# One decoder trunk step on one core: two convolution blocks as three pairs of column blocks, and half of the low parts by an accumulating transfer

## The chip, the core and the metric

The kernel runs on one core of a Trainium2 chip. A core has a matrix engine (TensorE, PE in the profile, with its weight loads as PEld), a vector engine (VectorE, DVE), an activation engine (ScalarE, ACT), a general engine (GpSimd, POOL) and a queue engine (SyncE, SP) that only starts transfers. Transfers run on 16 DMA engines; SP and POOL start nearly all of them here. The metric is the device time of one execution, in microseconds (us).

## What is computed

One step of a decoder layer for 512 prompt positions and 8 sample tokens, 520 columns in all, with a model width of 2048. The core of the reference:

```python
def mixer(xn, conv_prev, gla_prev, w_in, conv_w, gate_w2, gate_b, gla_norm_g, w_out, chunk):
    proj = xn @ w_in                       # 2048 -> 6160 columns
    bg, cg, hin, q, k, v, og, glr = jnp.split(proj, [_S1, _S2, _S3, _S4, _S5, _S6, _S7], axis=-1)
    cu, conv_new = causal_dwconv(cg * hin, conv_prev, conv_w)
    ya = bg * cu                           # 1024 channels of gated convolution
    logf = jax.nn.log_sigmoid((glr @ gate_w2 + gate_b).astype(f32)) / GATE_TAU
    o, s_new = gla_chunked(qh, kh, vh, lf, gla_prev.astype(f32), chunk)   # 4 heads
    ...
    yb = (o.reshape(Bn, L, GLA_V_DIM) * jax.nn.silu(og.astype(f32))).astype(xn.dtype)
    out = jnp.concatenate([ya, yb], axis=-1) @ w_out

def trunk(...):
    m, c_new, s_new = mixer(rmsnorm(x, norm_mix_g[l]), ...)
    x = x + m
    f, f_new = conv_ffn(rmsnorm(x, norm_ffn_g[l]), ...)   # 2048 -> 2 x 5632 -> 2048
    x = x + f
    return rmsnorm(x, final_norm_g), ...
```

The 1024 convolution channels are 8 blocks of 128. A block j needs three blocks of 128 columns of the input projection: one of cg, one of hin and one of bg.

## The kernel before

**Products in three parts.** All matrices are float32. A weight tile of 128 x 1024 (eight 128 x 128 pieces of one column block, 512 KB) is loaded as `raw`, rounded by ScalarE to `hi`, and VectorE subtracts `lo = raw - hi`. The activations are split likewise, and a product is hi x hi + lo x hi + hi x lo: three matmuls, each of 128 x 128 weights against 260 columns (half of the 520).

**Stages.** Up to about 59 us the input is transposed and split. Then comes the *plain stage*: column blocks of the input projection one after the other, each by `group()` (L213): 16 pieces in depth, three parts, two halves of the columns, 96 matmuls. After it comes the *pair stage*: two column blocks at once by a seven-product scheme (the products named in `ORDER`; sums of the weights and sums of the activations go in, and each of the seven products has half the depth and half the columns), 7 x 8 x 3 = 168 matmuls for what takes two plain groups 192. The output projection and the two FFN projections use the seven products as well.

**The plain stage** has 28 column blocks from 59 us on: the value blocks of head 0, four blocks (key, query, two of value) of each of heads 1 to 3 with one convolution block (`conv_tile`, three groups) behind each, the fourth convolution block, and two output-gate blocks (columns 5120 and 5248, in code of their own after the loop, L1797 to L1830). Within it the linear attention of a head is a generator (`gla_head`, L934). It is cut into small steps, and `group()` lets one step go at each of its *beats*, after the depth pieces named in `BEATS`: at 3, 7, 11 and 15. A step puts a few small matmuls between those of the group and gives VectorE, ScalarE and POOL the work that belongs to it. A level of the attention runs like this: POOL subtracts cumulative gates (`e`, L285), ScalarE takes the exponential (L984), VectorE multiplies with query and key into `L` (L991), TensorE forms scores of it (L1066), VectorE copies these into `at` (L1073). Products run two steps ahead of their scores and the subtractions three. `mixer_sums` (L774), another generator, prepares activation sums for the pair stage, one step at the end of each group.

**Weights of the plain stage.** Two halves (eight depth pieces each) make a block. `next_half()` (L205) takes a finished half and calls `high()` (L190), in which ScalarE makes the `hi` of the half that is used two halves later. Three pieces into the half, `low()` (L197) lets VectorE make its `lo`, and `fetch()` (L185) starts the load of the half three further on, from SP. Each of `raw`, `hi` and `lo` has three buffers, so a load waits until the `lo` of the half that had the buffer is made, and `hi` waits until TensorE is through with the half three before.

**Order.** In this part of the program every engine, with POOL's and SP's queues, keeps the order in which the code was written (`InOrder`, L885). An instruction that waits holds all behind it on its engine.

**The pair stage** goes through `MIX`: `ch` is the cg and hin blocks of one convolution block, `b` the bg blocks of two convolution blocks, `og` two output-gate blocks. Each pair takes `prepare` (L1355) for hi and lo of the weight sums, and one of the sums is made by an accumulating transfer from POOL's queue (`raw<-raw`, L1319). The results of convolution blocks are stored as `g_d`, from where the output projection loads them.

Of the kernel before, what the change touches and what calls it, by code (L numbers as in the profile page):

```python
# [17 lines left out]
P = 128  # L18
# [19 lines left out]
def trunk_kernel(  # L38
# [146 lines left out]
    def fetch():  # L185
        if ahead:
            k0, c0 = ahead.popleft()
            coming.append(load(w_in, k0, 8, c0, P))

    def high():  # L190
        if coming:
            raw, nk = coming.popleft()
            hi = wp.tile([P, 1024], F32R, tag="hi", name="hi")
            nc.scalar.activation(hi, raw, AF.Copy)
            highs.append((raw, nk, hi))

    def low():  # L197
        if highs:
            raw, nk, hi = highs.popleft()
            lo = wp.tile([P, 1024], F32R, tag="lo", name="lo")  # L200
            nc.vector.tensor_tensor(lo, raw, hi.bitcast(F32), op=ALU.subtract)
            halved.append([x.rearrange("p (k c) -> p k c", k=nk) for x in (hi, lo)])
            fetch()
# [7 lines left out]
    BEATS = (3, 7, 11, 15)  # L211

    def group():  # L213
        ps = new_mm()
        for k in range(KD):
            if k % 8 == 0:
                w = next_half()
            span(ps, w, xa, k, k // 8 * 8, 1, KD)
            if k in BEATS:
                beat()  # L220
            if k % 8 == 3:
                low()
        if extra and next(extra[0], extra) is extra:
            extra.popleft()
        return ps
# [548 lines left out]
    def mixer_sums():  # L774
# [38 lines left out]
        ("ch", 4), ("og", 2), ("ch", 5), ("og", 4), ("b", 4), ("og", 6), ("ch", 6), ("ch", 7),  # L813
        ("b", 6),
# [26 lines left out]
    with ExitStack() as mix:  # L841
# [44 lines left out]
        with ExitStack() as gl:  # L886
# [15 lines left out]
            for h in range(NH):  # L902
                tile_cols = (3584 + h * P, 3072 + h * P, 4096 + h * DV, 4096 + h * DV + P)
                for c0 in (*tile_cols, *(x + (h - 1) * P for x in (1024, 2048, 0)))[
                    slice(3, 4) if h == 0 else slice(None)
                ]:
                    ahead += [(0, c0), (8, c0)]
            ahead += [(k0, c0) for c0 in (1408, 2432, 384, 5120, 5248) for k0 in (0, 8)]
# [324 lines left out]
            for h in range(NH):  # L1233
                if h == 1:
                    extra.append(mixer_sums())
                ps = group() if h else None
# [3 lines left out]
                ps = group() if h else None  # L1240
# [23 lines left out]
                if h:  # L1264
                    conv_tile(h - 1)
            conv_tile(NH - 1)
# [838 lines left out]
```

## Time and profile before

| what | value |
|---|---|
| median of 3 runs | 2143.29 us (2142.72 to 2144.54) |
| the profiled execution's own time | 2143.29 us |
| its span, first to last instruction | 2141.5 us |
| granted TensorE clock, mean | 0.998 |
| TensorE busy | 2117.8 us, 99% |
| VectorE / ScalarE / POOL busy | 1747.0 / 1105.2 / 434.9 us |

The profiled execution is the median run. A matmul row of 281 ns is not the price of a matmul: matmuls overlap, and the price is the distance between their starts, which is read from the chain of waits or from the timeline. Stages are best told apart by a table of windows: it gives the busy time of each engine in each stretch, the granted clock, the share of the DMA engines, and what they moved.

### The profile page before, as it was taken

The numbers are of one execution on the slowest core, as the hardware profiler recorded it, in microseconds if no ns is written. First come the engines' busy times: TensorE is split into PE (matmuls) and PEld (weight loads), VectorE is DVE, ScalarE is ACT, GpSimd is POOL, SyncE is SP. The second block draws the span as 40 slices with busy tenths as digits, with TensorE's granted clock in tenths as the row PEclk, the third lists the DMA queues.
The fourth block names the chain that finished last, engine by engine and source line by source line (L and its number), as shares of the span: only waits on it lengthen the run. The fifth ranks groups of instructions, "written<-read, shape, count | busy, mean of one in ns | idle before, by whom it ended". The sixth has DMA issues, their size and how long they took to land.

```text
span 2141.5 us, 44283 instructions
## 1 busy us (share of the span) xinstructions
PE 2117.8 (99%) x17952; PEld 2097.2 (98%) x17952; DVE 1747.0 (82%) x2333; ACT 1105.2 (52%) x1662; POOL 434.9 (20%) x622
## 2 busy tenths in 40 slices
PE   9999999999999989999999999999999999999997
PEld 8999999999999989999999999999999999999997
DVE  6457576688979898998998988988989778888886
ACT  7434434355544686555555555555555554444445
POOL 4213223111334311111211221212212300200000
PEclk9999999999999999999999999999999999999999
DMA  8445473597898996676676676676676966994734
GB/s 257 129 134 176 132 206 114 147 253 187 223 287 239 267 287 164 173 190 177 179 185 174 181 184 174 180 187 175 178 188 180 298 203 163 276 291 133 225 109 159
DMA packets 467325, 415.74 MB, mean 194 GB/s; under 512 B 21721, under 2 KB 426473, under 8 KB 466977
## 3 DMA queue, kind: packets, MB, share of 16 engines
q1 hardware_dynamic: 424209, 289.84, 47.7%
q0 software_dynamic: 42864, 123.00, 21.9%
q8 instruction: 141, 2.31, 0.4%
q14 instruction: 63, 0.52, 0.1%
q10 hardware_dynamic: 48, 0.07, 0.0%
HBM read 299.65 MB, written 80.31 MB: 177 GB/s over the span
## 4 chain that ended last, share of the span: by engine, by line
PE 87%; DMA 5%; DVE 4%; issue 2%; POOL 1%; ACT 1%; SPq 1%; ACTq 0%; DVEq 0%; POOLq 0%
PE mm L1394 34%; PE mm L140 15%; PE ms L1394 14%; PE x L1637 7%; PE y L1637 7%; PE f L1637 3%; PE e L1637 3%; DVE lo L1374 1%; DMA x_d<-acc 1%; DMA form<-g_d 1%; DMA raw<-in_w_in_dram 1%; DMA wgraw<-in_w_in_dram 1%; DVE acc L1656 1%; PE ms L1066 1%; DMA g_d<-fh 0%
## 5 line engine op out<-in xcount | busy, mean ns | idle before, releaser
L1394 PE MATMUL mm<-yl,hi 128*128 128x260 f32 x1696 | 477.2, 281 | 3.5 <-DVE yl L124 3.5
L1394 PE MATMUL mm<-yh,hi 128*128 128x260 f32 x1696 | 475.9, 281 | 1.3 <-ACT ms L1404 0.7
L1394 PE MATMUL mm<-yh,lo 128*128 128x260 f32 x1696 | 475.3, 280 | 1.4 <-DVE lo L1374 1.4
L1370 ACT ACTIVATE hi<-raw 128x1024 fp32r<-128x1024 f32 x324 | 341.8, 1055 | 242.2 <-issue 90.1
L1374 DVE TENSOR_TENSOR lo<-raw,hi 128x1024 fp32r<-128x1024 f32 x324 | 396.1, 1222 | 44.3 <-ACT hi L1370 40.8
L1374 DVE TENSOR_TENSOR lo<-s,hi 128x1024 fp32r<-128x1024 f32 x243 | 298.5, 1228 | 124.4 <-ACT hi L1370 124.2
L1370 ACT ACTIVATE hi<-s 128x1024 fp32r<-128x1024 f32 x243 | 256.7, 1056 | 220.6 <-PE ms L1394 93.6
L1394 PEld LDWEIGHTS mm<-yl,hi 128*128 128x128 f32 x1696 | 318.9, 188 | 4.1 <-DVE yl L124 4.1
L1394 PEld LDWEIGHTS mm<-yh,lo 128*128 128x128 f32 x1696 | 319.9, 189 | 1.8 <-DVE lo L1374 1.8
L1394 PEld LDWEIGHTS mm<-yh,hi 128*128 128x128 f32 x1696 | 319.8, 189 | 1.7 <-ACT ms L1404 0.9
L1394 PE MATMUL ms<-b,hi 128*128 128x260 f32 x1408 | 265.7, 281 | 0.0
L1394 PEld LDWEIGHTS ms<-b,hi 128*128 128x128 f32 x1408 | 222.8, 189 | 0.0
L1637 PE MATMUL x<-form,hi 128*128 128x260 f32 x1120 | 211.8, 281 | 0.9 <-ACT f L1662 0.5
L1637 PE MATMUL y<-form,hi 128*128 128x260 f32 x1120 | 211.5, 281 | 0.0
L1315 DVE TENSOR_TENSOR s<-s,raw 128x1024 f32<-128x1024 f32 x162 | 198.0, 1222 | 2.8
L1394 PE MATMUL ms<-b,lo 128*128 128x260 f32 x704 | 197.4, 280 | 0.0
L1637 PEld LDWEIGHTS x<-form,hi 128*128 128x128 f32 x1120 | 176.5, 188 | 1.7 <-issue 0.8
L1637 PEld LDWEIGHTS y<-form,hi 128*128 128x128 f32 x1120 | 176.5, 188 | 0.3
L1637 PE MATMUL x<-form,lo 128*128 128x260 f32 x560 | 157.0, 280 | 0.4 <-DVE lo L1374 0.4
L1637 PE MATMUL y<-form,lo 128*128 128x260 f32 x560 | 156.8, 280 | 0.0
L1394 PEld LDWEIGHTS ms<-b,lo 128*128 128x128 f32 x704 | 132.4, 188 | 0.0
L1394 PE MATMUL mm<-bh,hi 128*128 128x260 f32 x424 | 118.8, 280 | 1.0 <-DVE acc L1656 1.0
(402 smaller groups left out, 5005.1 us busy)
## 6 DMA issues: line engine op xcount, KB each, us to landing
raw<-in_w_up_dram SPq DMA_DIRECT2D x176, 512.0 KB, 5.1
raw<-in_w_down_dram SPq DMA_DIRECT2D x96, 512.0 KB, 5.6
raw<-in_w_in_dram SPq DMA_DIRECT2D x92, 512.0 KB, 4.3
form<-f_d SPq DMA_DIRECT2D x126, 260.0 KB, 6.1
raw<-raw POOLq DMA_DIRECT2D x56, 512.0 KB, 5.9
f_d<-t POOLq DMA_DIRECT2D x80, 260.0 KB, 5.5
raw<-in_w_out_dram SPq DMA_DIRECT2D x32, 512.0 KB, 9.3
form<-g_d POOLq DMA_DIRECT2D x42, 260.0 KB, 7.6
```

What stands on the lines that cost most here:

```text
L140: nc.tensor.matmul(o, w, xx, start=first and i == 0, stop=last and i == 2)
L1066: nc.tensor.matmul(pb[t, c * 32 : (c + 1) * 32], L[:, c, t], second(L[:, c : c + 1, t])[:, 0], start=True, stop=True, tile_position=(0, t. ...
L1315: return lambda: nc.vector.tensor_tensor(out, x, y, op=ALU.add)
L1370: nc.scalar.activation(his[i], src, AF.Copy)
L1374: nc.vector.tensor_tensor(los[i], src, his[i].bitcast(F32), op=ALU.subtract)
L1394: nc.tensor.matmul(st["bank"][b], w[:, k, :], x, start=b not in st["used"] and k == 0 and j == 0, stop=k == 7 and j == 2, skip_group_check ...
L1637: nc.tensor.matmul(ps[:, m, :], w[:, k, m * P : (m + 1) * P], x, start=b not in st["used"] and k == 0 and j == 0, stop=k == 3 and j == 2, ...
L1656: nc.vector.tensor_tensor(a, a, inner(bk[b]), op=op)
```

## The change

Four things change together.

- Convolution blocks 2 and 3 leave the plain stage, which so has 22 column blocks in place of 28. They come back as three pairs at the head of `MIX`: `ch` 2, `ch` 3 and `b` 2. Blocks 0 and 1 stay plain and stand together behind head 3.
- `BEATS` has five entries (2, 5, 8, 11, 14), so the steps of a head come after three depth pieces in place of four, and a head's steps are spread over four groups and a little.
- `mixer_sums` goes on twice in the key and query groups, in the middle and at the end.
- For the second half of each block (`k0 == 8`, 21 halves in all) VectorE makes no `lo`. ScalarE writes the negative of `hi` into the `lo` buffer right after `hi`, and POOL starts a transfer that adds `raw` to it.

```diff
--- before.py
+++ after.py
@@ -185,20 +185,26 @@
     def fetch():
         if ahead:
             k0, c0 = ahead.popleft()
-            coming.append(load(w_in, k0, 8, c0, P))
+            coming.append((*load(w_in, k0, 8, c0, P), k0 == 8))
 
     def high():
         if coming:
-            raw, nk = coming.popleft()
+            raw, nk, by_dma = coming.popleft()
             hi = wp.tile([P, 1024], F32R, tag="hi", name="hi")
             nc.scalar.activation(hi, raw, AF.Copy)
-            highs.append((raw, nk, hi))
+            lo = None
+            if by_dma:
+                lo = wp.tile([P, 1024], F32R, tag="lo", name="lo")
+                nc.scalar.activation(lo, hi.bitcast(F32), AF.Copy, scale=-1.0)
+                nc.gpsimd.dma_start(lo.bitcast(F32), raw, accum_op=ALU.add)
+            highs.append((raw, nk, hi, lo))
 
     def low():
         if highs:
-            raw, nk, hi = highs.popleft()
-            lo = wp.tile([P, 1024], F32R, tag="lo", name="lo")
-            nc.vector.tensor_tensor(lo, raw, hi.bitcast(F32), op=ALU.subtract)
+            raw, nk, hi, lo = highs.popleft()
+            if lo is None:
+                lo = wp.tile([P, 1024], F32R, tag="lo", name="lo")
+                nc.vector.tensor_tensor(lo, raw, hi.bitcast(F32), op=ALU.subtract)
             halved.append([x.rearrange("p (k c) -> p k c", k=nk) for x in (hi, lo)])
             fetch()
 
@@ -208,9 +214,13 @@
         high()
         return w
 
-    BEATS = (3, 7, 11, 15)
-
-    def group():
+    BEATS = (2, 5, 8, 11, 14)
+
+    def further():
+        if extra and next(extra[0], extra) is extra:
+            extra.popleft()
+
+    def group(twice=False):
         ps = new_mm()
         for k in range(KD):
             if k % 8 == 0:
@@ -220,8 +230,9 @@
                 beat()
             if k % 8 == 3:
                 low()
-        if extra and next(extra[0], extra) is extra:
-            extra.popleft()
+            if k == 7 and twice:
+                further()
+        further()
         return ps
 
 
@@ -810,8 +821,8 @@
 
 
     MIX = (
-        ("ch", 4), ("og", 2), ("ch", 5), ("og", 4), ("b", 4), ("og", 6), ("ch", 6), ("ch", 7),
-        ("b", 6),
+        ("ch", 2), ("og", 2), ("ch", 3), ("og", 4), ("b", 2), ("ch", 4), ("og", 6), ("ch", 5),
+        ("b", 4), ("ch", 6), ("ch", 7), ("b", 6),
     )
 
     def mix_source(n, m, k):
@@ -899,13 +910,12 @@
                     base=-32 * j, pattern=[[-1, NS]], channel_multiplier=1,
                 )
             w2s = gp.tile([96, 512], F32R, name="w2s")
-            for h in range(NH):
-                tile_cols = (3584 + h * P, 3072 + h * P, 4096 + h * DV, 4096 + h * DV + P)
-                for c0 in (*tile_cols, *(x + (h - 1) * P for x in (1024, 2048, 0)))[
-                    slice(3, 4) if h == 0 else slice(None)
-                ]:
-                    ahead += [(0, c0), (8, c0)]
-            ahead += [(k0, c0) for c0 in (1408, 2432, 384, 5120, 5248) for k0 in (0, 8)]
+            cols = [4096 + P]
+            for h in range(1, NH):
+                cols += [3584 + h * P, 3072 + h * P, 4096 + h * DV, 4096 + h * DV + P]
+            for j in range(2):
+                cols += [1024 + j * P, 2048 + j * P, j * P]
+            ahead += [(k0, c0) for c0 in (*cols, 5120, 5248) for k0 in (0, 8)]
             halved += v0
             for _ in range(3):
                 fetch()
@@ -1233,11 +1243,11 @@
             for h in range(NH):
                 if h == 1:
                     extra.append(mixer_sums())
-                ps = group() if h else None
+                ps = group(True) if h else None
                 k = gp.tile([P, T], F32, tag="qk", name="k", bufs=5)
                 if h:
                     evac(ps, k)
-                ps = group() if h else None
+                ps = group(True) if h else None
                 assert done[0] >= h - 1
                 q = gp.tile([P, T], F32, tag="qk", name="q", bufs=5)
                 if h:
@@ -1261,9 +1271,8 @@
                     soon.append(lambda t=t, vt=vt, d=d: v_rows(t, vt, d, 0, 4))
                 soon.append(lambda v=v, h=h: v_samples(v, h))
                 queue.append(gla_head(h, q, k, vt))
-                if h:
-                    conv_tile(h - 1)
-            conv_tile(NH - 1)
+            for j in range(2):
+                conv_tile(j)
             for _ in range(3):
                 side.popleft()()
             assert not queue and not extra and not soon, (len(queue), len(extra), len(soon))
```

The first place where the order moves is POOL's queue within a head's levels. These are its rows before, from head 0's second level on (`e`: the subtractions of a level, one row for each):

```order
L285 TENSOR_TENSOR e<-bc 128x8x32 x2
L285 TENSOR_TENSOR e<-bc 128x16x16 x2
L285 TENSOR_TENSOR e<-bc 128x32x8 x2
L285 TENSOR_TENSOR e<-bc 128x64x4 x2
L285 TENSOR_TENSOR e<-bc 128x128x2 x2
```

And now (L199 is the accumulating transfer):

```order
L296 TENSOR_TENSOR e<-bc 128x8x32 x2
L199 DMA lo<-raw 128x1024
L296 TENSOR_TENSOR e<-bc 128x16x16 x2
L296 TENSOR_TENSOR e<-bc 128x32x8 x2
L296 TENSOR_TENSOR e<-bc 128x64x4 x2
```

A transfer that waits for ScalarE's negative `hi` now stands between the subtractions of two levels.

The second place is POOL's queue where the plain stage ends and the pair stage begins. `o_d` is head 3's result, `g_d_120` the stores of the last two plain convolution blocks, `g_d_119` those of the first output gates. Before:

```order
L1195 DMA o_d<-o 128x520 x2
L740 DMA g_d_120<-t 128x260
L740 DMA g_d_120<-zpad_855 128x260
L740 DMA g_d_120<-t 128x2x260 x6
L740 DMA g_d_119<-fh 128x260
```

And now:

```order
L199 DMA lo<-raw 128x1024
L1205 DMA o_d<-o 128x520 x2
L751 DMA g_d_120<-t 128x260
L751 DMA g_d_120<-zpad_855 128x260
L751 DMA g_d_120<-t 128x2x260 x6
L199 DMA lo<-raw 128x1024
L751 DMA g_d_119<-fh 128x260
```

The `lo` of the last half of the plain stage (the second half of column block 5248), which VectorE made before, now stands behind eight stores in POOL's queue.

## The prediction

> **What bounds the kernel now.** I read the page's busy times and its chain of waits first, then the table of windows by stage, then what TensorE waited for.
>
> ```profile
> span 2141.5 us, 44283 instructions
> PE 2117.8 (99%) x17952; PEld 2097.2 (98%) x17952; DVE 1747.0 (82%) x2333; ACT 1105.2 (52%) x1662; POOL 434.9 (20%) x622
> PE 87%; DMA 5%; DVE 4%; issue 2%; POOL 1%; ACT 1%; SPq 1%; ACTq 0%; DVEq 0%; POOLq 0%
> ```
>
> TensorE is busy for 99% of the span and holds 87% of the chain that ended last. A matmul removed is time removed, as long as nothing else comes to wait. The windows say where room for that is. The first row is the plain stage, the second the pair stage, the third where the two meet; the columns are the length, the busy times of PE, PEld, DVE, ACT and POOL, the clock, the share of the DMA engines and GB/s.
>
> ```profile
> 59.00:437.50 378.50, 378.25 (x3425) 366.08 (x3426) 230.87 (x401) 159.24 (x264) 90.36 (x112) 1.00 0.53 153
> 437.50:621.00 183.50, 180.66 (x1510) 179.66 (x1509) 165.24 (x216) 99.00 (x148) 44.38 (x66) 1.00 0.82 220
> 433.00:460.00 27.00, 24.16 (x194) 23.16 (x194) 24.55 (x35) 16.95 (x27) 1.10 (x2) 1.00 0.90 263
> ```
>
> In the plain stage VectorE is busy for 61% (230.87 of 378.50), ScalarE for 42%, and the DMA engines have half their time free. In the pair stage VectorE stands at 90%. Where they meet TensorE is idle for 2.8 us of 27, with VectorE at 91%: the weakest place. In the whole plain stage TensorE waited once, for 0.2 us:
>
> ```profile
> PE ms L1134 <- DVE at L1073: 0.2, 1, 0.2
> ```
>
> **The change, part by part.** *Fewer matmuls.* The price of one is read from the chain, where starts follow each other without a gap: 144 plain matmuls in one piece, and three starts of the same product of successive pairs.
>
> ```profile
> 307.00 17.17 PE mm L140 x144
> ...
> 499.38 11.41 PE mm L1394 x96
> 519.37 11.41 PE mm L1394 x96
> 539.36 5.71 PE mm L1394 x48
> ```
>
> A plain matmul costs 17.17 / 144 = 0.119 us, a plain group of 96 costs 11.45 us. A pair costs 519.37 - 499.38 = 19.99 us with all that it brings. Out go six groups, 6 x 11.45 = 68.7 us; in come three pairs, 3 x 19.99 = 60.0 us. That is **-8.7 us** (72 matmuls fewer). The pair price holds if new pairs run like these: `ch 2, og 2, ch 3` repeats the old beginning with other numbers, and `ch 5, b 4` stand next to each other as `ch 7, b 6` did already. The small matmuls of the heads are the same in number; they only go to other places.
>
> *Low parts by transfer.* Here are the durations: ScalarE's `hi`, VectorE's `lo`, POOL's issue of an accumulating transfer of the same size in the pair and FFN stages, its median time to landing, and the load of a `raw` in the plain stage.
>
> ```profile
> L194 ACT ACTIVATE hi<-raw x54: 1040/1050/1080, 52.8 to 420.5; 128x1024 fp32r<-128x1024 f32 x54
> L201 DVE TENSOR_TENSOR lo<-raw,hi x54: 1209/1220/2123, 54.0 to 421.6; 128x1024 fp32r<-128x1024 f32 x54
> L1319 POOL DMA_DIRECT2D raw<-raw x56: 847/906/952, 461.1 to 1651.2; - x56
> raw<-raw POOLq DMA_DIRECT2D x56, 512.0 KB, 5.9
> raw<-in_w_in_dram SPq DMA_DIRECT2D x55, 512.0 KB, 4.1
> ```
>
> 21 times 1.22 us = 26 us leave VectorE, 21 x 1.05 = 22 us come to ScalarE, which has over 200 us free in the stage, and 21 x 0.91 = 19 us to POOL, which is at 24%. The negative `hi` isn't in the trace; I give it the price of `hi`, the same engine and shape (bounds: half of it and twice it). A `lo` then is there 1.05 + 1.05 + 0.91 + 5.9 = 8.9 us after its half's turn on ScalarE begins. It is needed a whole group later, 11.45 us without a head's steps and about 14.5 us with five of some 0.6 us each (the score rows below). So it is in time by 2.5 to 5.6 us: 0 us. The `raw` buffer comes free at 8.9 us instead of some 5; the next load lands at about 13 us, needed three halves later, at 17. SP's queue stands behind that load until then, and a head's sample loads behind SP; where these were late before, it was ScalarE that waited, and TensorE not:
>
> ```profile
> L1025 ACT ACTIVATE vb<-vb,k 128x256 f32<-128x256 f32 x32 | 14.4, 498 | 13.0 <-DMA vb<-v_d 8.8 <-DVE lo L201 3.6 <-DVE at L1073 0.6
> ```
>
> *Five steps per group.* Between two steps lie 18 matmuls in place of 24, 2.15 us for 2.86. The tightest place of the chain inside a head shows in VectorE's and TensorE's timelines (start, length):
>
> ```profile
> 271.39 0.43 DVE L991 TENSOR_TENSOR L<-e,q 128x256 f32<-128x256 f32 x1
> 271.73 0.42 DVE L991 TENSOR_TENSOR L<-e,k 128x256 f32<-128x256 f32 x1
> 272.07 1.66 DVE L1028 SCALAR_TENSOR_TENSOR s<-s,asm,vb 128x256 f32<-128x256 f32 x2
> 273.76 0.63 DVE L1073 COPY_PREDICATED at<-mask,ms 64x128 f32<-64x128 uint8 x2
> 274.42 1.01 DVE L991 TENSOR_TENSOR L<-e,q 128x256 f32<-128x256 f32 x1
> 275.35 1.50 DVE L991 TENSOR_TENSOR L<-e,k 128x256 f32<-128x256 f32 x1
> ```
> ```profile
> 274.50 0.66 PE L1066 MATMUL ms<-L 128*64 128x32 f32 x16
> ...
> 278.71 0.66 PE L1066 MATMUL ms<-L 128*64 128x32 f32 x16
> ```
>
> ```profile
> L991 DVE TENSOR_TENSOR L<-e,k x28: 410/420/1912, 91.9 to 372.4; 128x256 f32<-128x256 f32 x28
> ```
>
> The products that ended at 272.15 are used at 274.50, those of 276.85 at 278.71: 2.35 and 1.86 us ahead. Products lie two steps ahead, so the closer steps take 2 x 0.71 = 1.4 us of it and leave 0.4 us at the worst place. But these groups also lose work that stood in VectorE's queue just there: the convolution blocks between the heads (now behind head 3) and every second `lo`. Bounds: 0 and, if each of the 28 score steps (one for each pair of products in the last row) were 0.6 us late, 17 us. I take **+0.5 us**, near the lower end, since the row of TensorE's waits has one wait of 0.2 us in all four heads. `mixer_sums` at twice the rate puts more into ScalarE and VectorE per group; both have the room of the first window.
>
> *Where the stages meet.* Head 3, the stores of the last plain convolution blocks and the first loads of the pair stage come together here. These rows are of ScalarE, POOL, TensorE, the transfers of this stretch, the chain, and the window.
>
> ```profile
> 420.53 1.06 ACT L194 ACTIVATE hi<-raw 128x1024 fp32r<-128x1024 f32 x1 [0.89 <-ACT t L123]
> ...
> 434.24 1.06 ACT L1370 ACTIVATE hi<-raw 128x1024 fp32r<-128x1024 f32 x1 [6.69 <-DMA raw<-in_w_in_dram]
> ```
> ```profile
> 418.81 4.26 POOL L740 DMA_DIRECT2D g_d<-t  x6
> ```
> ```profile
> 431.99 0.40 PE L140 MATMUL mm<-xh,lo 128*128 128x260 f32 x2
> ```
> ```profile
> g_d<-t POOLq DMA_DIRECT2D x6, 260.0 KB, 8.5
> ```
> ```profile
> 421.17 12.97 DMA raw<-in_w_in_dram
> ```
> ```profile
> 424.00:434.00 10.00, 10.00 (x86) 10.00 (x85) 1.99 (x3) 0.64 (x1) 0.00 (x0) 1.00 1.08 301
> ```
>
> The last half's `hi` starts at 420.53; its negative is done at 422.6. In POOL's queue the new transfer stands behind the stores, whose issue ends at 423.07, and is issued by 424.0. TensorE wants this `lo` at 431.99. With 5.9 us it lands at 429.9, in time; with the 8.5 us of the stores in the same queue and stretch it lands at 432.5, 0.5 us late; with its own half megabyte at the 301 GB/s that the full DMA engines moved there (1.7 us more), 2.2 us late. Those 1.7 us also push the first weight load of the pair stage, which took 12.97 us as it is. ScalarE waited for it until 434.24, and VectorE is full from there on, so its delay reaches TensorE. The two delays overlap in time, and I take the larger of the likely ones, **+1.7 us**. Bounds: both in full and one behind the other, +3.9 us; and a gain of 1.2 us, since VectorE has one `lo` less to make just before its full stretch.
>
> One rule is weighed here. The Trainium skill, page "DMA: Bandwidth & Descriptors", section "Anatomy of one DMA — SWDGE (gpsimd) path", gives a transfer issued from GpSimd a fixed 2.0 us plus its bytes at 436 GB/s. For 512 KB that is an estimate of 3.2 us, against the 5.9 us of the row; with it the last `lo` would land at 427.2, nothing would wait, and the sum would be 2135.1 us. With the row the sum is the one below, and I go by the row.
>
> *Sum*, against the profiled execution's own 2143.29 us (span 2141.5, 1.8 us around it), which is also the median: 2143.29 - 8.7 + 0.5 + 1.7 = **2136.8 us**.
>
> **Rivals.** *All of the saving arrives.* The transfers land in time at the meeting place too, and VectorE's relief there offsets the crowding: 2143.29 - 8.7 = 2134.6 us; with the 1.2 us as well, 2133.4. For it: landing margins of 2 us and more by the median. Against it: the DMA share of 1.08 there.
>
> *The meeting place takes half of it back.* The last `lo` and the first weight load are both late in full, 3.9 us, and VectorE's full stretch, in which TensorE is idle for 2.8 us already, repeats as much once more, since delayed activation sums are split by ScalarE and VectorE in order: 2143.29 - 8.7 + 0.5 + 3.9 + 2.8 = 2141.8 us, within 0.2% of before. For it: the 12.97 us of one load. Against it: a TensorE that is late itself waits less afterwards.
>
> *The heads become the bound (slower).* One mechanism, in POOL's queue: the new transfer stands between the subtractions of two levels and waits for ScalarE's second pass, 2.1 us into the half. The subtraction behind it comes later by up to 2.1 + 0.9 us, then the exponential, then the products, and a score waits on TensorE with all behind it. It decides once products are late by more than the 0.4 us that the closer steps leave. At 0.6 us for each of 28 scores it costs 17 us: 2143.29 - 8.7 + 17 + 1.7 = 2153 us; at 0.4 us each it is still 2147.5. For it: products that took 1.01 and 1.50 us in place of 0.42. Against it: subtractions run three steps ahead, about 8.4 us, and only one or two transfers fall into a head's levels.
>
> *The change does not do what it says*: the added transfers land later than a group, so each of 21 halves waits. That needs over 11.45 us for 8.9; only the meeting place shows such times. At 1 us each that would be 2157 us.
>
> **How the numbers follow.** Forecast 0.44, all of the saving 0.26, half taken back 0.17, heads as the bound 0.10, late everywhere 0.03. The predicted time is 2136.8 us. What a measurement of this kernel can tell from no change is about 0.2%, 4.3 us: under 2139.0 is faster, over 2147.6 slower. The forecast's own range is 2134 to 2139. The range runs from 2133 (the saving with VectorE's relief) to 2143 (past the half taken back), and leaves out the slower cases and a little at the low end. Faster: 0.42 + 0.26 + 0.02 = 0.70; same: 0.02 + 0.15 + 0.02 = 0.19; slower: the rest, 0.11.
>
> **What would show it.** In the profile of the changed kernel the number of matmuls falls by 72. The plain stage ends about 69 us earlier, at some 369 us, and the pair stage lasts 60 us longer, with pairs 19.99 us apart. Accumulating transfers into `lo` land in about 6 us, and TensorE shows no waits for `lo` but one of up to 2 us in the last plain half. TensorE's waits for `L` or `at` in the plain stage stay under 1 us in sum. The forecast is wrong if those waits exceed 4 us, if TensorE is idle for over 6 us in the 27 us where the stages meet, or if pairs are farther apart than 20 us.

## The result, and the profile after

The changed kernel takes 2151.43 us (median of ten runs, 2146.12 to 2156.40); the kernel before, run beside it, 2144.35 us. The ratio is 1.0034, with an interval of 1.0024 to 1.0044: slower by 7.1 us, where 6.5 us faster was forecast (2143.29 to 2136.8). The profiled execution spans 2148.8 us against 2141.5.

The page of the changed kernel, its length and busy times:

```profile
span 2148.8 us, 44276 instructions
PE 2112.5 (98%) x17880; PEld 2090.1 (97%) x17880; DVE 1745.0 (81%) x2328; ACT 1143.6 (53%) x1709; POOL 447.9 (21%) x644
```

The 72 matmuls are gone (17880 for 17952), and TensorE is busy 5.3 us less, in a span that is 7.3 us longer. So the matrix work went away as planned, and more idle time came than it had saved. Where it came is told by the first matmul of the pair stage. These are the rows of its `b` products in the groups of TensorE's matmuls (shortest, median and longest duration, then the first and last start), of before and of the change:

```profile
L1394 PE MATMUL mm<-bh,hi x424: 278/280/358, 437.5 to 1657.2; 128*128 128x260 f32 x142
```
```profile
L1403 PE MATMUL mm<-bh,hi x448: 278/280/353, 385.3 to 1664.5; 128*128 128x260 f32 x150
```

The plain stage ends 437.5 - 385.3 = 52.2 us earlier. Six groups are 68.7 us, so 16.5 us were lost inside it. From there to the end of the span it is 2148.8 - 385.3 = 1763.5 us for 2141.5 - 437.5 = 1704.0: the three new pairs cost 59.5 us, as forecast (60.0). All of the net loss is in the plain stage. What TensorE waited for there (total, times and longest, in us), in the changed kernel, leaving out one wait of 0.3 us; before the change this stage had one wait of 0.2 us:

```profile
PE ms L1149 <- DVE S L1160: 3.6, 2, 2.6
PE ms L1076 <- DVE L L1001: 2.8, 3, 1.4
PE mm L140 <- DMA lo<-raw: 2.0, 1, 2.0
PE ms L641 <- POOL t L296: 1.8, 1, 1.8
PE ms L1132 <- POOL kc L296: 1.3, 1, 1.3
PE ms L1144 <- ACT vt L931: 1.0, 1, 1.0
```

That is 12.5 us in nine waits: nearly all kinds of side work of the heads are late, each a little. `S` is the head's running state, `L` the products for a score, `t` the sum of squares in a head's norm, `kc` the decayed keys, `vt` the transposed values. `lo<-raw` is the last plain half, at the place where the stages meet.

The longest of them, of head 0, followed back through the timeline of the changed kernel (SP's, ScalarE's, VectorE's and TensorE's rows):

```profile
119.78 0.50 SPq L1029 DMA_DIRECT2D vb<-v_d  x1
...
125.30 0.91 ACT L1035 ACTIVATE vb<-vb,k 128x256 f32<-128x256 f32 x2 [6.14 <-DMA vb<-v_d]
...
125.84 0.88 DVE L1038 SCALAR_TENSOR_TENSOR s<-s,asm,vb 128x256 f32<-128x256 f32 x2 [6.78 <-ACT vb L1035]
126.76 0.42 DVE L1160 COPY S<-ms 128x256 f32<-128x256 f32 x1
...
127.24 0.49 PE L1149 MATMUL ms<-qb,S 128*128 128x128 f32 x2 [2.60 <-DVE S L1160]
```

A sample load (`vb`) is issued at 119.78 and lands 5.5 us later. ScalarE waits for it for 6.14 us, VectorE's sample update waits for ScalarE, the copy of `S` stands behind that update in VectorE's queue, and TensorE stands still for 2.60 us. Two steps lie between the issue and the use. With four steps per group ScalarE waited for this load in one head, and TensorE in none; with five steps TensorE waits too.

The wait for `kc` comes from another queue. These are ScalarE's and POOL's rows a little earlier in the same head:

```profile
112.68 0.62 ACT L1121 ACTIVATE kc<-kc 128x512 f32<-128x512 f32 x1
...
114.27 1.06 ACT L198 ACTIVATE lo<-hi 128x1024 fp32r<-128x1024 f32 x1
...
115.63 0.89 POOL L199 DMA_DIRECT2D lo<-raw  x1 [4.90 <-ACT lo L198]
116.25 1.56 POOL L296 TENSOR_TENSOR kc<-kc,k 128x512 f32<-128x512 f32 x1
```

`kc` is ready for POOL at 113.3, but ahead of it in POOL's queue stands the new transfer, which waits for ScalarE's negative until 115.3. POOL is idle for 4.90 us and starts on `kc` 2.9 us late.

One more thing is in the windows of the changed kernel (length, busy times of PE, PEld, DVE, ACT and POOL, clock, share of the DMA engines, GB/s), right behind the wait of 2.60 us:

```profile
128.00:130.00 2.00, 2.00 (x14) 0.89 (x13) 2.00 (x5) 0.77 (x2) 0.00 (x0) 0.67 0.93 226
130.00:132.00 2.00, 2.00 (x11) 2.00 (x10) 0.60 (x1) 0.00 (x0) 0.00 (x0) 0.50 0.54 132
132.00:134.00 2.00, 2.00 (x20) 2.00 (x19) 0.00 (x0) 0.47 (x1) 0.00 (x0) 0.98 0.85 242
```

TensorE counts as busy, but at half its clock: 2 x (0.33 + 0.50 + 0.02) = 1.7 us more are lost, which no row of waits shows. With them 14.2 of the 16.5 us have a name; for the other 2.3 no single row was found.

### The profile page after: what moved, and what is told of

It is laid out like the page before. It is cut to its first block, busy times and chain, and to the rows that moved or that the text cites. A ratio compares the mean times of both kernels' runs of the same rounds, so it can differ in the third digit from the quotient of the medians.

```text
span 2148.8 us, 44276 instructions
## 1 busy us (share of the span) xinstructions
PE 2112.5 (98%) x17880; PEld 2090.1 (97%) x17880; DVE 1745.0 (81%) x2328; ACT 1143.6 (53%) x1709; POOL 447.9 (21%) x644
## 4 chain that ended last, share of the span: by engine, by line
PE 88%; DMA 5%; DVE 4%; issue 1%; ACT 1%; SPq 1%; POOL 0%; ACTq 0%; DVEq 0%; POOLq 0%
PE mm L1403 36%; PE ms L1403 14%; PE mm L140 12%; PE x L1646 8%; PE y L1646 8%; PE e L1646 3%; PE f L1646 3%; DMA raw<-in_w_out_dram 1%; DVE lo L1383 1%; DMA ssq<-fh 1%; DMA wgraw<-in_w_in_dram 1%; DMA vb<-v_d 1%; DVE s L1038 0%; PE ms L2004 0%; DMA R<-fh 0%
## 5 line engine op out<-in xcount | busy, mean ns | idle before, releaser
L1403 PE MATMUL mm<-yl,hi 128*128 128x260 f32 x1792 | 504.8, 282 | 2.6 <-DVE yl L124 2.6
L1403 PE MATMUL mm<-yh,hi 128*128 128x260 f32 x1792 | 503.3, 281 | 1.4 <-ACT ms L1413 1.3
L1403 PE MATMUL mm<-yh,lo 128*128 128x260 f32 x1792 | 502.7, 281 | 1.0 <-DVE lo L1383 1.0
L1379 ACT ACTIVATE hi<-raw 128x1024 fp32r<-128x1024 f32 x336 | 354.4, 1055 | 249.0 <-issue 88.8
L1383 DVE TENSOR_TENSOR lo<-raw,hi 128x1024 fp32r<-128x1024 f32 x336 | 410.3, 1221 | 42.7 <-ACT hi L1379 38.7
L1383 DVE TENSOR_TENSOR lo<-s,hi 128x1024 fp32r<-128x1024 f32 x252 | 309.4, 1228 | 131.7 <-ACT hi L1379 131.5
L1379 ACT ACTIVATE hi<-s 128x1024 fp32r<-128x1024 f32 x252 | 266.4, 1057 | 229.5 <-PE ms L1403 97.3
L1403 PEld LDWEIGHTS mm<-yl,hi 128*128 128x128 f32 x1792 | 337.4, 188 | 3.5 <-DVE yl L124 3.5
L1403 PEld LDWEIGHTS mm<-yh,hi 128*128 128x128 f32 x1792 | 338.4, 189 | 1.8 <-ACT ms L1413 1.5
L1403 PEld LDWEIGHTS mm<-yh,lo 128*128 128x128 f32 x1792 | 338.5, 189 | 1.3 <-DVE lo L1383 1.2
```

Source lines behind the costliest of these rows:

```text
L1379: nc.scalar.activation(his[i], src, AF.Copy)
L1383: nc.vector.tensor_tensor(los[i], src, his[i].bitcast(F32), op=ALU.subtract)
L1403: nc.tensor.matmul(st["bank"][b], w[:, k, :], x, start=b not in st["used"] and k == 0 and j == 0, stop=k == 7 and j == 2, skip_group_check ...
```

## The experiments

Two theories stood at the start. **A**: the transfer is the price, since it holds POOL's queue and ScalarE's second pass holds ScalarE's. **B**: the five steps are the price, since the last sample load of a head comes too late. Each run is given as its median, beside that of the kernel before on the same chip; since the latter lies between 2142.69 and 2144.35 from one set of runs to the next, runs are compared with each other by their differences from it. Each interval is about 1 part in 1000 to either side, some 2 us, so two runs that differ by 2 to 3 us are hardly told apart by their times.

| run | us | before | difference | ratio (interval) |
| --- | --- | --- | --- | --- |
| the change | 2151.43 | 2144.35 | +7.1 | 1.0034 (1.0024 to 1.0044) |
| the change, every `lo` by VectorE | 2137.96 | 2142.97 | -5.0 | 0.9978 (0.9969 to 0.9987) |
| the change, early sample loads | 2144.70 | 2142.97 | +1.7 | 1.0009 (1.0000 to 1.0018) |
| before, five steps | 2151.19 | 2142.97 | +8.2 | 1.0039 (1.0026 to 1.0052) |
| before, transfers | 2143.34 | 2142.97 | +0.4 | 1.0004 (0.9995 to 1.0013) |
| the change, VectorE and early loads | 2136.73 | 2142.69 | -6.0 | 0.9970 (0.9959 to 0.9982) |
| the change, transfers issued later | 2145.34 | 2142.69 | +2.7 | 1.0008 (0.9999 to 1.0017) |
| the same with early loads | 2142.53 | 2142.69 | -0.2 | 0.9995 (0.9986 to 1.0003) |
| before, five steps and early loads | 2142.57 | 2142.69 | -0.1 | 0.9999 (0.9990 to 1.0008) |
| later, early, last half by VectorE | 2140.22 | 2143.00 | -2.8 | 0.9986 (0.9977 to 0.9995) |
| the same, second pass later too | 2142.85 | 2143.00 | -0.2 | 0.9998 (0.9989 to 1.0007) |
| VectorE, early loads, mixer later | 2135.27 | 2143.00 | -7.7 | 0.9964 (0.9950 to 0.9978) |
| VectorE, early loads, second pass kept | 2140.01 | 2143.60 | -3.6 | 0.9984 (0.9975 to 0.9993) |

### Every low part by VectorE again

```diff
-            coming.append((*load(w_in, k0, 8, c0, P), k0 == 8))
+            coming.append((*load(w_in, k0, 8, c0, P), False))
```

> The changed kernel, but all low parts of the plain stage are made by VectorE as before: no negative hi by ScalarE, no accumulating transfer. Theory A (the transfer and ScalarE's second pass stand in POOL's and ScalarE's order ahead of a head's levels, and make levels, sample states and sums late): TensorE's waits in the plain stage fall from 15 us to under 3 us and the time comes to 2136 to 2139 us, faster than before. Theory B (five steps per group are too close for the loads of the sample states and for the products, whoever makes the low parts): the waits stay above 9 us, the time stays at 2147 to 2152 us.

2137.96 us: 5.0 under the kernel before, 12.1 better than the change. The waits of the plain stage that are left, but for one of 0.3 us:

```profile
PE ms L1149 <- DVE S L1160: 2.0, 1, 2.0
PE ms L1076 <- DVE L L1001: 1.9, 2, 1.7
PE ms L641 <- POOL t L296: 0.8, 1, 0.8
```

The waits for `kc`, `vt` and `lo<-raw` are gone. The fewer matmuls do save time, and in this arrangement the transfer costs more than they save.

### The last sample load two steps earlier

```diff
-                    s0 = gp.tile([P, 2, DV], F32, tag="s0", name="s0", bufs=3)
+                    s0 = gp.tile([P, 2, DV], F32, tag="s0", name="s0", bufs=4)
...
-                    if i in (0, 2, 5):
-                        loaded.append(sample_load({0: 2, 2: 4, 5: 6}[i]))
+                    if i in (0, 2, 3):
+                        loaded.append(sample_load({0: 2, 2: 4, 3: 6}[i]))
```

Beside it three small edits make room for the fourth `s0`: one mask is no longer made, `vss` shares the buffer of `os`, and `asm` has one buffer in place of two.

> The changed kernel, with the last load of a head's sample states two steps earlier (a fourth buffer for them, room for which comes from buffers that nothing else fills at that time). Theory A: the waits on ScalarE for vb (6.1 and 4.5 us in the trace) fall away and with them 4 to 5 us of TensorE's waits, but the late kc, the late sum of squares and the late L remain: 2145 to 2148 us. Theory B: the loads were the cause, 2139 to 2143 us.

2144.70 us, 1.7 over the kernel before and 5.4 better than the change. `S` and `vt` have left the waits; the others stay as they were:

```profile
PE ms L1077 <- DVE L L1002: 2.8, 3, 1.4
PE ms L642 <- POOL t L296: 1.8, 1, 1.8
...
PE ms L1133 <- POOL kc L296: 1.2, 1, 1.2
```

So the late load is one cause and not the only one.

### The kernel before, with five steps alone

```diff
-    BEATS = (3, 7, 11, 15)
+    BEATS = (2, 5, 8, 11, 14)
```

> The kernel before with five steps per group (2, 5, 8, 11, 14) and nothing else: blocks 2 and 3 still plain between the heads, all low parts by VectorE. Theory A: 2143 to 2146 us, no change that matters. Theory B: the closer steps alone bring the waits on sample loads and on L: 2148 us and more.

2151.19 us, 8.2 over the kernel before: without any transfer and without any moved block. Its longest waits, then the last sample load of head 0 at its issue (SP) and at its use (ScalarE):

```profile
PE ms L1139 <- DVE S L1150: 7.1, 3, 2.9
```
```profile
115.24 1.62 SPq L1019 DMA_DIRECT2D vb<-v_d  x1
...
119.86 0.91 ACT L1025 ACTIVATE vb<-vb,k 128x256 f32<-128x256 f32 x2 [2.47 <-DMA vb<-v_d]
```

### The kernel before, with five steps and the early load

The edits of the two runs above together.

> The kernel before with five steps and the last sample load two steps earlier. If the late sample load is all that five steps cost (2151.19 us without the earlier load, 7.1 us of waits for S), the waits for S are gone and the time is that of the kernel before, 2143 to 2144.5 us. If five steps also make products or sums late, waits for L or at of 2 us and more take their place, and it is 2147 to 2151 us.

2142.57 us, no different from before (0.9990 to 1.0008). The same two rows, and the longest wait that is left in the plain stage:

```profile
107.81 0.46 SPq L1020 DMA_DIRECT2D vb<-v_d  x1
...
115.90 0.90 ACT L1026 ACTIVATE vb<-vb,k 128x256 f32<-128x256 f32 x2
```
```profile
PE ms L1135 <- DVE at L1074: 1.3, 1, 1.3
```

The load is issued 8.1 us ahead of its use in place of 4.6, and ScalarE doesn't wait. That settles the price of five steps in this arrangement: it was the late sample load, all 8 us of it. The products and scores, which the prediction had looked at, are fast enough for five steps.

### The kernel before, with the transfers alone

`fetch`, `high` and `low` as in the change, four steps and the old order of blocks.

> The kernel before with every second low part by ScalarE and the accumulating transfer (27 halves) and nothing else: four steps per group, all convolution blocks where they were. Theory A: the queues are held up here too, 2147 to 2152 us, with waits on kc, sums or sample states. Theory B: steps 3.7 us apart leave room, 2142 to 2146 us.

2143.34 us, no different from before (0.9995 to 1.0013), with one wait in the plain stage:

```profile
PE mm L140 <- DMA lo<-raw: 2.7, 1, 2.7
```

With four steps the transfers cost nothing in the heads. Neither theory is enough by itself: A's part costs nothing alone, B's costs 8 us alone, and with five steps and the moved blocks the transfer costs 12.1 us. The parts do not add up: -8.7 us for fewer matmuls, +8.2 and +0.4 make -0.1, and the change stands at +7.1.

### VectorE's low parts and the early load together

> The changed kernel with every lo by VectorE and the last sample load of each head two steps earlier. If the transfer's price and the late sample load are two separate causes, their gains add: the first of them alone gave 2137.96 us and had 2.0 us of TensorE's waits for S left, with a window of half clock behind it worth 1.7 us, so 2134.3 us here, and no wait for S. If the two are one cause (the transfer is what makes the load late), the early load brings nothing more: 2138 us.

2136.73 us, between the two expectations and nearer to the second. `S` has left the waits (`L` 2.0 and `t` 0.8 us are left). The early load brings 5.4 us with the transfers and 1.0 without, an amount that the intervals don't tell from nothing. So the two gains do not add. One reason may be in the traces: with the transfers in flight the load itself takes longer. This is the last load of head 0 in the kernel with every `lo` by VectorE, to be read beside the same load of the change (issued at 119.78, used at 125.30):

```profile
117.89 0.50 SPq L1029 DMA_DIRECT2D vb<-v_d  x1
...
122.62 0.91 ACT L1035 ACTIVATE vb<-vb,k 128x256 f32<-128x256 f32 x2 [4.46 <-DMA vb<-v_d]
```

Here it can be used 4.7 us after its issue, in the change 5.5. (TensorE still waits 2.0 us for `S` there, since VectorE's own `lo`, 1.22 us from 123.96 on, stands ahead of the copy of `S`.) That this 0.8 us makes the whole difference between 5.4 and 1.0 is not shown; the profile tells the landing of only one or two of the 16 sample loads in each of these traces.

### The transfer issued three pieces later

```diff
                 nc.scalar.activation(lo, hi.bitcast(F32), AF.Copy, scale=-1.0)
-                nc.gpsimd.dma_start(lo.bitcast(F32), raw, accum_op=ALU.add)
...
                 nc.vector.tensor_tensor(lo, raw, hi.bitcast(F32), op=ALU.subtract)
+            else:
+                nc.gpsimd.dma_start(lo.bitcast(F32), raw, accum_op=ALU.add)
```

> The changed kernel with its accumulating transfers issued three pieces later in their half, where ScalarE's negative is already there. If what costs is POOL standing still at the transfer for ScalarE, with kc and a head's subtractions behind it, the waits for kc (1.3 us) and vt (1.0) go and those for L (2.8) shrink below 1: 2151.4 - 5 = 2146 us, though the wait for the last lo grows from 2.0 to some 5 us, which may give 3 us back: 2149. If what costs is the second pass on ScalarE itself, the waits for t (1.8) and S (3.6) and L stay, and only the last lo gets worse: 2151 to 2155 us.

2145.34 us, 2.7 over the kernel before and 4.4 better than the change, from moving one issue. POOL's `kc` of head 0, and what TensorE still waits for:

```profile
110.32 1.52 POOL L297 TENSOR_TENSOR kc<-kc,k 128x512 f32<-128x512 f32 x1 [1.73 <-ACT kc L1122]
```
```profile
PE ms L1150 <- DVE S L1161: 2.2, 2, 1.2
PE ms L1077 <- DVE L L1002: 2.2, 3, 1.1
...
PE mm L140 <- DMA lo<-raw: 1.0, 1, 1.0
```

`kc` now starts as soon as ScalarE has finished it, and the wait for it is gone. So the place of the issue is a cause, worth about 4 us. That all of it is POOL standing still is not shown: the wait for `kc` makes 1.3 us, and those for `S` (3.6 to 2.2 us), `L` and `lo` fell as well. In two places the expectation was wrong: the wait for `L` only fell from 2.8 to 2.2, and the last `lo` came earlier against its use, not later. Its issue had stood behind the stores of the convolution blocks in POOL's queue anyway, and still does.

### Issued later, with the early load

> The kernel before this one with the last sample load of each head two steps earlier. Against the changed kernel with the early load alone (2144.7 us) it tells the same two theories apart where no load is late: if POOL standing still is the price, the waits for L and kc go (4.0 us) and the time is 2140 to 2142 us; if it is ScalarE's second pass, it is 2144 to 2148 us. If the transfer's cost is its traffic against the sample loads, it is 2144.7 us again with the waits of a head unchanged.

2142.53 us, the kernel before again (0.9986 to 1.0003). Of 8.7 us that the fewer matmuls should bring, nothing is left over yet.

### The last half's low part by VectorE

```diff
-            coming.append((*load(w_in, k0, 8, c0, P), k0 == 8))
+            coming.append((*load(w_in, k0, 8, c0, P), k0 == 8 and c0 != 5248))
```

> The kernel with the transfers issued later and the early sample loads (2142.53 us), and the low part of the last plain half by VectorE instead of by transfer. If that transfer's wait at the meeting place (1.4 us there, 2.0 in the changed kernel) is simply lost time, it goes: 2141 us. If VectorE's full stretch right behind makes another wait of it, the wait only moves: 2142.5 us or more.

2140.22 us, 2.8 under the kernel before and 2.6 better than with the last transfer. The wait at the meeting place is gone and none has come in its place, so it was simply lost time. How much is open: the wait was 1.4 us, and the intervals of the two kernels overlap.

### ScalarE's second pass later as well

```diff
             if by_dma:
-                lo = wp.tile([P, 1024], F32R, tag="lo", name="lo")
-                nc.scalar.activation(lo, hi.bitcast(F32), AF.Copy, scale=-1.0)
+                lo = True
...
             else:
+                lo = wp.tile([P, 1024], F32R, tag="lo", name="lo")
+                nc.scalar.activation(lo, hi.bitcast(F32), AF.Copy, scale=-1.0)
                 nc.gpsimd.dma_start(lo.bitcast(F32), raw, accum_op=ALU.add)
```

> The kernel before this one, with ScalarE's second pass, the negative of hi, also three pieces later, so that it no longer stands directly behind the first pass. If the second pass holding ScalarE's queue for 2.1 us in a piece is what remains between the transfer and VectorE's lo, the wait for t falls from 1.8 us to the 0.8 that VectorE's lo leaves, and the time is 1 to 3 us under the kernel before this: 2138 to 2140 us. If the transfers now land too late (needed a group later, about 3 us less in hand), waits for lo from a transfer show at many halves and it is 2143 us or more.

2142.85 us, 2.6 worse than without this edit (the intervals overlap); neither expectation holds as it stood:

```profile
PE ms L1079 <- DVE L L1004: 3.3, 2, 2.6
...
PE mm L140 <- DMA lo<-raw: 1.1, 1, 1.1
PE ms L644 <- POOL t L298: 0.8, 1, 0.8
```

The wait for `t` did fall from 1.8 to 0.8, but a wait of 2.6 us for `L` has come in another place, and one transfer now lands 1.1 us late. The pass of a microsecond seems to be in some head's way in both positions; that it makes the wait for `L` was not tested.

### The second pass without the transfer

In the kernel with the later issue and the early load, VectorE writes `raw - hi` over ScalarE's negative, where the transfer was issued:

```diff
             else:
-                nc.gpsimd.dma_start(lo.bitcast(F32), raw, accum_op=ALU.add)
+                nc.vector.tensor_tensor(lo, raw, hi.bitcast(F32), op=ALU.subtract)
```

> The kernel with every lo by VectorE and the early sample loads (2136.73 us), in which ScalarE still writes the negative of hi for every second half, directly behind hi, and VectorE then writes raw - hi over it: ScalarE's second pass without the transfer. If what remains of the transfer's price (2140.22 us with VectorE for the last half alone) is ScalarE's time, the wait for t is back at 1.8 us and the time is 2138.5 to 2140.5 us. If it is POOL's issue and the traffic, the time is 2136.7 us and the wait for t stays at 0.8.

2140.01 us, 3.6 under the kernel before: 2.4 worse than without the pass (the two intervals overlap a little), and level with the 2.8 for the transfers without the last one. The waits:

```profile
PE ms L1078 <- DVE L L1003: 3.1, 2, 1.8
PE ms L643 <- POOL t L297: 1.8, 1, 1.8
```

The wait of 1.8 us for `t` is back without any transfer. So ScalarE's second pass makes this wait, and by the times it may make most of what was left of the transfer's price; since the intervals overlap, that much is likely and not shown. In the change the pass is `hi` at 275.41, the negative at 276.50, and behind them on ScalarE what the head waits for:

```profile
275.41 1.06 ACT L194 ACTIVATE hi<-raw 128x1024 fp32r<-128x1024 f32 x1 [1.47 <-PE mm L140]
276.50 1.06 ACT L198 ACTIVATE lo<-hi 128x1024 fp32r<-128x1024 f32 x1
...
278.26 0.62 ACT L1188 ACTIVATE t<-o 128x520 f32<-128x520 f32 x1
```

### The mixer's sums later

In the kernel with VectorE's low parts and the early load, the doubled steps of `mixer_sums` stand in the groups of head 1 and of the convolution blocks, in place of heads 1 to 3:

```diff
-                ps = group(True) if h else None
+                ps = group(h == 1) if h else None
...
         def conv_tile(j):
-            ps = group()
+            ps = group(True)
```

(each in two places)

> The fastest kernel so far (every lo by VectorE, early sample loads, 2136.73 us), with four of the six doubled steps of the mixer's sums moved from the groups of heads 2 and 3 to the convolution blocks behind head 3. If these sums are what makes the products L late in head 2 (2.0 us of waits, with a window of half clock behind them), those waits go: 2133 to 2134.5 us. If they are late for another reason (the order of hi and the exponential on ScalarE), the waits stay and it is 2136.7 us; if the sums now crowd the place where the stages meet, it is above 2138 us.

2135.27 us, the fastest of all, 0.9964 (0.9950 to 0.9978) of the kernel before. It can't be told from the 2136.73 without the edit. `L` is still waited for 2.0 us, so the sums were not the main reason for its lateness. The profiled execution with the edit has no stretch of half clock before its last 12 us, the one without has one, and such a stretch costs 1.7 us (last section): the gap between the two gains, 7.7 and 6.0 us, is about as large. The first `b` product of the pair stage starts at 371.0, where the forecast had the plain stage end at "some 369":

```profile
L1404 PE MATMUL mm<-bh,hi x448: 278/281/352, 371.0 to 1650.1; 128*128 128x260 f32 x150
```

## Why the prediction was wrong

**Fewer matmuls, -8.7 us: right.** 72 matmuls fewer, three pairs for 59.5 us, and 7.7 us of it arrive in the fastest variant (2143.00 to 2135.27).

**Low parts by transfer, 0 us: wrong, 12.1 us in this arrangement.** The step asked when a `lo` is there and when it is needed, and that was answered rightly (its 8.9 us holds the 0.91 of the issue twice, since a row's time to landing counts from the start of the issue, but that errs on the safe side): the 21 transfers land in 5.4 us by the median, and TensorE waits for one `lo` only. It did not ask what stands behind the new instructions in their queues. It weighed ScalarE's 22 us and POOL's 19 us against free time summed over the whole stage ("over 200 us free"), and a head's chain passes through both queues in order. The runs take the price apart, one edit after the other: 4.4 us for the issue at which POOL stands until ScalarE's negative is done; 2.8 for the last sample load; 2.6 for the last half; 3.2 for the rest, of which the negative alone makes 2.4. That is 13.0 us, from the change at +7.1 to -6.0. The shares hang on the order of the edits (the early load brings 5.4 us when it comes first, and 1.0 when it comes last), and by the intervals of the table only the first is clear of the noise.

**Five steps, +0.5 us: wrong, 8.2 us when made alone.** The step priced the products, found 0.4 us of margin, and stayed near the lower end. Those waits were indeed small when five steps came alone (`at` 1.2 us). The failing sentence is the one on the sample loads: "where these were late before, it was ScalarE that waited, and TensorE not". The profile of before showed ScalarE waiting 8.8 us for `vb`; that was the last reserve of a chain that ends in `S` on TensorE, and closer steps used it up. With the load two steps earlier the five steps cost nothing. In the changed arrangement, with every `lo` by VectorE, their price is smaller: -5.0 of the -8.7 us arrives, so five steps, the moved blocks and the doubled steps of the sums cost 3.7 us together there.

**The meeting place, +1.7 us: about right, in part by luck.** The last `lo` was 2.0 us late, for 0.5 to 2.2 forecast, and TensorE is idle for 4.3 us in the 27 us from 377 on, where it was 2.8 before (from 433 on). Two waits of 1.3 and 1.0 us a little later, in the first pair, are followed by half clock at 394.9, which costs 1.7 us more (last section). The transfer took 11.0 us from the start of its issue to landing. From there the forecast's two cases are 0.91 + 8.5 = 9.4 us and, with 1.7 more, 11.1, which fits; but here too the 0.91 stands in them twice, and without it the first case lands in time and the second 1.3 us late, not 2.2. The 1.7 us of the sum was meant for the first weight load of the pair stage. ScalarE did wait for that longer than before, 9.54 us for 6.69, and the wait that shows on TensorE is the one for the `lo`:

```profile
368.59 0.94 POOL L199 DMA_DIRECT2D lo<-raw  x1
```
```profile
DMA to landing us min/median/max: 4.5/5.4/11.0
```

The Trainium skill's fit, page "DMA: Bandwidth & Descriptors", section "Anatomy of one DMA — SWDGE (gpsimd) path", by which this is an estimate of 3.2 us for 512 KB, lies below the fastest of the 21; it was right to go by the row, 5.9.

**The rivals.** "The heads become the bound", with a chance of 0.10, came nearest: that a transfer holds up POOL's queue is in the rows above. That its price of 2147.5 to 2153 us holds 2151.43 is luck: it counted 28 late scores of 0.4 to 0.6 us, and the trace has three waits for `L` of 2.8 us in all. It placed the mechanism on the subtractions and scores, and the runs show it on `kc`; a second mechanism that no rival had, the sample loads, makes 5.4 us of the 14.6 between forecast and result. The argument that set its chance so low, subtractions running three steps ahead, says nothing on `kc`, `t` and `vb`, which run one or two steps ahead.

**What would show it.** Neither of two conditions for a wrong forecast was met by its letter: waits for `L` or `at` over 4 us (`L` 2.8), and over 6 us idle in the 27 us where the stages meet (4.3). The loss came in the waits for `S`, `t`, `kc` and `vt`, which the list did not have.

## What to carry to other kernels

Before work is moved to an engine with free time, read what stands behind the new instructions in that engine's queue at the tightest place, not its share of busy time: an issue that waits for another engine holds everything behind it, and moving it to where its input is already there was worth 4 us here. When the steps of a chain move closer together, price every transfer that is issued a fixed number of steps ahead; an engine that waits for such a transfer in the profile of before, even at no cost, has no reserve left. Make the parts of a change alone as well as together: one part cost nothing alone and 12 us together with the others.

## What the hardware showed that was not expected

A wait of some 2 us on TensorE can cost nearly as much again, since the granted clock falls to a half behind it for 3.4 us (the windows of the change above). The matmuls of the kernel with VectorE's low parts and the early load show it (start and length, one form):

```profile
307.90 0.40 PE L140 MATMUL mm<-xh,lo 128*128 128x260 f32 x2
...
310.29 0.66 PE L1077 MATMUL ms<-L 128*64 128x32 f32 x16 [1.75 <-DVE L L1002]
...
313.36 0.64 PE L140 MATMUL mm<-xh,lo 128*128 128x260 f32 x2
...
315.54 0.40 PE L140 MATMUL mm<-xh,lo 128*128 128x260 f32 x2
```

The same two matmuls take 0.40 us ahead of the wait of 1.75 us, 0.64 behind it, and 0.40 again 2 us later. A wait of the same length in the kernel with the later issue and the early load has no such stretch behind it; its row, and the window that follows:

```profile
270.49 1.15 PE L643 MATMUL ms<-t,ones 128*128 128x260 f32 x4 [1.81 <-POOL t L297]
```
```profile
272.00:280.00 8.00, 8.00 (x69) 8.00 (x69) 6.29 (x11) 3.52 (x7) 0.00 (x0) 1.00 0.57 134
```

So the length of the wait alone does not decide. The Trainium skill, page "TensorE: Matmul & The Clock Gate", section "What's actually happening", tells of a free-running window of 3413 ns, which would make it depend on where the wait falls in that window. The traces agree on the window. Every stretch of half clock in them but the one at the end of a span lasts 3.4 us, and where a trace has more than one, their starts lie whole multiples of 3.413 us apart: 266.24 us in the change (128.67 and 394.91, 78 times), 191.15 with every `lo` by VectorE (56 times), 102.40 in the kernel before with five steps (30 times). These are windows of the change laid on that grid, the last one ahead of the second stretch, and the stretch:

```profile
391.50:394.91 3.41, 1.26 (x8) 1.06 (x9) 3.41 (x6) 3.25 (x7) 0.00 (x0) 1.00 1.21 293
394.91:398.32 3.41, 3.41 (x18) 3.41 (x18) 3.41 (x5) 1.55 (x2) 0.00 (x0) 0.50 0.54 117
```

TensorE is busy for 1.26 of 3.41 us, 37%, in the window ahead. Over the twelve traces with such a stretch, between 20 and 2110 us, each of the 15 windows of the grid with TensorE busy for less than 46.8% was followed by half clock. Of the eight from 46.8 to 52.2% three were, and of the fuller ones none. So in these traces waits cost clock when they take more than some 1.8 us of one window (53% of 3.41, an estimate from these shares). The wait of 2.00 us for the last `lo` in the change straddles the edge at 377.85 and has no stretch behind it, though it is longer than the one of 1.75 us that has. The two waits of 1.75 and 1.81 us above both lie whole inside one window, busy for 46.2% where the clock falls and for 46.8% where it does not: close to the limit, and where they fall does not tell them apart. This is read off the traces, in which busy times of TensorE are modelled; no run was made to test it. The same page, section "Why this matters for your kernels", warns of idle gaps over some 3 us; here 1.75 us were enough. Whether these stretches also make the ten runs of the change spread over 10 us, where the ten of before spread over 5, stays open.
